# Scores of the first token tile with both key halves side by side, and rotary scores with the halves stacked on the partitions

## The chip, the cores and the metric

The kernel runs on one core of a Trainium2 chip. The core has five engines that work at the same time and wait for each other by semaphores: TensorE (PE; matmuls and transposes into PSUM), VectorE (DVE), ScalarE (ACT), GpSimd (POOL) and SyncE (SP, which here only starts transfers). Results of TensorE land in PSUM, which has eight banks of 128 partitions by 512 values; everything else is kept in SBUF. The metric is the device time in microseconds (us), the median of several runs.

## The reference

A decoder trunk of two layers over 256 tokens (one sequence, model width 2048), all in float32. Layer 0 is differential attention: 16 heads in pairs, each of 128 values per head, partial rotation, two softmaxes per pair whose difference weighs the values. Layer 1 is latent attention: queries and keys come out of low-rank projections; each of 16 heads has 128 unrotated values and 64 rotated ones, and the rotated key is one for all heads. Both are causal. After each of them comes a cross attention into 256 memory tokens and a squared-ReLU MLP of width 8192; a final norm closes the trunk. What matters here:

```python
# layer 0, per pair of heads
s = jnp.einsum('bqhcd,bkhcd->bhcqk', qi, k).astype(jnp.float32) * scale
s = jnp.where(causal_mask(q0, S), s, -jnp.inf)
p = jax.nn.softmax(s, axis=-1)
a = (p[:, :, 0] - lam * p[:, :, 1]).astype(v.dtype)
...
# layer 1
k_rope = apply_rope(d[..., MLA_Q_LORA + MLA_KV_LORA:][:, :, None, :], cos, sin)
q = jnp.concatenate([q[..., :MLA_NOPE], apply_rope(q[..., MLA_NOPE:], cos, sin)], axis=-1)
k = jnp.concatenate([kv[..., :MLA_NOPE],
                     jnp.broadcast_to(k_rope, (B, S, MLA_HEADS, MLA_ROPE))], axis=-1)
s = jnp.einsum('bqhd,bkhd->bhqk', qi, k).astype(jnp.float32) * scale
```

## The kernel before

**Precision.** Every operand of a float32 product is kept as two halves, a high one (the value rounded by a cast) and a low one (the rest, by a subtraction). A product is three matmuls into one PSUM bank: high by high, high by low, low by high. ScalarE makes the high half and VectorE the low half: of weights on lines 193 and 194 (`whi`, `wlo`, tiles of 128 x 1024, a ring of four buffers each, so that a cast waits until TensorE has used up an older weight), of activations in `split` (lines 296 and 297, tiles `unit`).

**Tiling.** The 256 tokens are two token tiles of 128, t = 0 and t = 1. The second tile sees 256 keys, the first one 128. Attention is worked in four groups of four heads (layer 0: four components, which is two pairs). A group is a Q, K and V projection, then scores, softmax, transposes of the probabilities, the weighted values, and the output projection of the group, which lies in the order behind the next group's start.

**Order of the work.** TensorE's order is written out by hand. The projections, which stream the weights, are the main line; scores, softmax, transposes are side tasks: generators that yield how long the next step should be put off (`T_ROT` = 12.0 for a rotation, `T_SM` = 6.5 for a softmax, `T_EV` = 2.6 for an evacuation), on a clock of the program's own to which each matmul adds its cost. `pump` runs between two pieces of the main line and takes a side step that is due; `need` runs side tasks until an operand exists. A side task that needs a PSUM bank takes one of four by `side_bank` and returns it with `give_back`. The order on VectorE, ScalarE, GpSimd and SyncE is set by the scheduler of the build, not by hand.

**Scores and softmax.** `scores` (line 530) writes the scores of four blocks of 128 keys (first tile) or two of 256 keys into one bank; VectorE adds the causal mask in place (line 541) and takes the maximum (line 511, `nmax`), ScalarE does the exponentials and row sums into an SBUF tile `p` (line 513), VectorE the reciprocal (line 518). In layer 1 (`attend4`) VectorE multiplies `p` by it (line 552), TensorE transposes `p` (line 159), and the transposes are split. In layer 0 (`attend_diff`) VectorE scales the two softmaxes of a pair into `a` (lines 641 and 642), and TensorE transposes `a`. The `ev` tiles, of which there are seven buffers, hold `p` and evacuated projections.

**The rotary part of layer 1.** `rotated` in `project_latent` evacuates the 64 rotary values of four heads by ScalarE (line 456, 128 x 256), GpSimd rotates them in place by six operations (`rope`, lines 467 to 472), TensorE turns two heads at a time (4 transposes for both token tiles), and `split` makes the halves. Two heads then lie one above the other on the partitions; the key `krope`, made by `shared_key`, has a copy for the upper and one for the lower position, with zeros in the other. So each rotary score is three products as well. The query projection and its evacuation (line 456, 128 x 512) follow the rotary projection, the transposes of the query follow these.

Of the kernel before, what the change touches and what calls it, by code (L numbers as in the profile page):

```python
# [10 lines left out]
F32 = mybir.dt.float32  # L11
# [6 lines left out]
P = 128  # L18
# [27 lines left out]
def trunk(ctx, tc, x, xT, xT0, mem, memT, positions, gcols, gfinal, lam_vecs, consts, W, out):  # L46
# [16 lines left out]
    def nm(s):  # L63
        serial[0] += 1
        return f"{s}_{serial[0]}"
# [104 lines left out]
    def raw_tile():  # L170
        return wraw.tile([P, 4 * CH], F32, tag="raw", name=nm("raw"))
# [333 lines left out]
    def softmax(sb, n):  # L505
# [4 lines left out]
        pr = work.tile([P, CH], F32, tag="ev", name=nm("p"), bufs=EVS)  # L510
        nc.vector.tensor_reduce(nmax[:, :n], sb.rearrange("p (n k) -> p n k", n=n), AX.X, ALU.max, negate=True)  # L511
        for i in range(n):
            nc.scalar.activation(  # L513
                pr[:, i * w : (i + 1) * w], sb[:, i * w : (i + 1) * w], AF.Exp,
                bias=nmax[:, i : i + 1], accum_out=ssum[:, i : i + 1],
            )
# [13 lines left out]
    def scores(sb, blocks, nk, t, causal):  # L530

        m = len(blocks)
        view = sb[:, : m * nk].rearrange("p (m k) -> p m k", m=m)
        for b, pairs in enumerate(blocks):
            n = len(pairs)
            for i, (q, qi, mh, ml) in enumerate(pairs):
                qs = slice(t * P, (t + 1) * P)
                mm3(view[:, b], q[:, 0, qi, qs], q[:, 1, qi, qs], mh, ml, i == 0, i == n - 1)
        if causal:
            last = view[:, :, nk - P :]  # L540
            nc.vector.tensor_tensor(last, last, mask.unsqueeze(1).broadcast_to([P, m, P]), ALU.add)

    def attend4(score_pairs, inputs, v, dst, causal):

# [1 line left out]
        pTs = [raw_tile().bitcast(F32R).rearrange("p (a b c d) -> p a b c d", a=2, b=2, c=2) for _ in range(2)]  # L546

        def probs(t, heads, nk):
            sb = yield from side_bank()
            scores(sb, [score_pairs(h, nk) for h in heads], nk, t, causal)  # L550
            pr, rs = softmax(sb, len(heads))
            nc.vector.tensor_tensor(
                pr.rearrange("p (h k) -> p h k", k=nk), pr.rearrange("p (h k) -> p h k", k=nk),
                rs[:, : len(heads)].unsqueeze(2).broadcast_to([P, len(heads), nk]), ALU.mult,
            )
# [69 lines left out]
    def attend_diff(q, k, v, dst, coef, subcols):  # L625


        def block(t, heads, out):
            nk = (t + 1) * P
            sb = yield from side_bank()  # L630
            comps = [s for h in heads for s in (2 * h, 2 * h + 1)]
            scores(sb, [[(q, s, k[:, 0, s, :nk], k[:, 1, s, :nk])] for s in comps], nk, t, True)
            n = 2 * len(heads)
            pr, rs = softmax(sb, n)
            nc.vector.tensor_tensor(rs[:, :n], rs[:, :n], coef[:, :n], ALU.mult)
            a = work.tile([P, S], F32, tag="a", name=nm("a"))
            for i in range(len(heads)):
                p0 = pr[:, 2 * i * nk : (2 * i + 1) * nk]
                p1 = pr[:, (2 * i + 1) * nk : (2 * i + 2) * nk]
                ai = a[:, i * nk : (i + 1) * nk]  # L640
                nc.vector.tensor_scalar(ai, p1, rs[:, 2 * i + 1 : 2 * i + 2], None, ALU.mult)
                nc.vector.scalar_tensor_tensor(ai, p0, rs[:, 2 * i : 2 * i + 1], ai, ALU.mult, ALU.add)
# [457 lines left out]
    def cross(l, norm, m, mk):  # L1100
        a = norm.done()
        rq = keep2(norm.rstd, SC_CA, "rq")
        q = Held(unit())
        ps = matmul_chunk(a)
        for t in range(NT):
            heads_T(ps[t], t, rq[t], q)
        o = Held(unit())
        mv = []
        attend4(
            lambda h, nk: [(q, h, mk[:, 0, h, :], mk[:, 1, h, :])], q.tasks + mk.tasks,  # L1110
            lambda: mv[0] if mv else None, o, False,
        )
        mv.append(mem_values(m))
        return project_out([o], G_MLP + 16 * l)
# [118 lines left out]
    acts = norm.done()  # L1233
    rk = keep2(norm.rstd, 1.0, "r1")
    hm = MLA_ROPE // 2
    krope = Held(raw_tile().bitcast(F32R)[:, : 4 * S].rearrange("p (a k t) -> p a k t", a=2, k=2))
    LAT = 3 * P

    def latent_piece(es, at, ps, lo, n):
# [35 lines left out]
    for t in range(NT):  # L1275
        e = work.tile([P, 2, P], F32, tag="a", name=nm("kr"))
        nc.vector.memset(e, 0.0)
        nc.scalar.activation(e[:, 0, 0:64], ps[t][:, 2 * P : 2 * P + 64], AF.Copy, scale=rk[t])
        ropes.append(e)
    ckv, rs = latent(ekv, G_KV)  # L1280
    rkv = keep2(rs, 1.0, "rkv")
# [1 line left out]
    def shared_key():  # L1283
        for t in range(NT):
            e = ropes[t]
            rope(e[:, 0:1, 0:64], cos[:, t, hd:], sin[:, t, hd:], 1, hm)
            nc.vector.tensor_copy(e[:, 1, 64:128], e[:, 0, 0:64])
        yield T_ROT
        b = yield from side_bank()
        for t in range(NT):  # L1290
            pt = b[:, 2 * t * P : 2 * (t + 1) * P]
            for i in range(2):
                flip(pt[:, i * P : (i + 1) * P], ropes[t][:, i, :])
        for t in range(NT):
            split(krope, t, b[:, 2 * t * P : 2 * (t + 1) * P].rearrange("p (k t) -> p k t", k=2))
        give_back()
        yield T_TURN

    def project_latent(gi):
        qr, q, k, v = Held(unit()[:, :, :2]), Held(unit()), Held(unit()), unit()  # L1300
        ps = matmul_chunk([cq], 256)

        def rotated(ps):
            es = []
            for t in range(NT):
                e = evacuate(ps[t][:, :256], rq[t])
                rope(e[:, :256].rearrange("p (h d) -> p h d", h=4), cos[:, t, hd:], sin[:, t, hd:], 4, hm)
                es.append(e)
            yield T_ROT
            b = yield from side_bank()  # L1310
            for t in range(NT):
                pt = b[:, 2 * t * P : 2 * (t + 1) * P]
                for i in range(2):
                    flip(pt[:, i * P : (i + 1) * P], es[t][:, i * P : (i + 1) * P])
            for t in range(NT):
                split(qr, t, b[:, 2 * t * P : 2 * (t + 1) * P].rearrange("p (k t) -> p k t", k=2))
            give_back()
            yield T_TURN

        qr.run(rotated(ps))  # L1320
# [139 lines left out]
```

## Time and profile before

| | us |
|---|---|
| median of 3 runs | 2239.43 (2238.33 to 2239.86) |
| profiled execution | 2237.86 |
| its span | 2236.1 |
| TensorE busy | 2215.5 (99%) |
| VectorE busy | 1744.0 (78%) |
| ScalarE busy | 1360.7 (61%) |
| GpSimd busy | 131.7 (6%) |

The granted TensorE clock was 0.999 over the span. In the rows of the profile PE, DVE, ACT, POOL and SP are the engines and L155 is line 155 of the kernel before. A row of the timeline has the start in us, the busy time, engine, line, operation, output tile <- input tiles, shapes and how many instructions follow each other (x12); in square brackets stands the idle time of the engine before it and what ended it. A row of the waits has an engine, line and tile, what it waited for, and the sum in us, the number of times and the longest. A row by form has the busy time, the mean duration in ns of one, and the idle time before. Consecutive matmuls overlap, so a duration is longer than the distance from one start to the next. Groups of layer 0 lie in the first 372 us (the fourth one's first tile at 346 to 361 us), those of layer 1 between about 1225 and 1420 us, the four groups' projections of the query at 1240, 1268, 1325 and 1378 us.

### The profile page before, as it was taken

The page shows a single profiled execution, that of the slowest core. Times are in us where ns is not written, and L with a number is a line of the kernel's source. Part 1 is how long each engine was busy: PE and PEld are TensorE (multiplying, and loading weights), DVE is VectorE, ACT ScalarE, POOL GpSimd, SP SyncE. Part 2 cuts the span into 40 slices and gives each one's busy share as a digit, 9 for nine tenths or more (in the row PEclk, how much of TensorE's full clock was granted, in tenths as well). Part 3 has the DMA queues.
Part 4 walks back from the last instruction along what each step waited for, and adds up shares of the span by engine and source line. Part 5 has one row for each costly group of instructions (what it writes and reads, how often), then busy time and mean ns, then how long its engine had stood idle before and what let it go on. Part 6 is the DMA issues. An engine that isn't in the chain of part 4 may idle for free.

```text
span 2236.1 us, 27352 instructions
## 1 busy us (share of the span) xinstructions
PE 2215.5 (99%) x10477; PEld 1847.1 (83%) x10477; DVE 1744.0 (78%) x1916; ACT 1360.7 (61%) x1815; POOL 131.7 (6%) x222
## 2 busy tenths in 40 slices
PE   9999999999999999999999999999999999999998
PEld 7888888888878888888889888888888888888886
DVE  6665748779889888889865767778988988898874
ACT  7544546666666666666655655566766666666664
POOL 1101010000000000000000311000000000000001
PEclk9999999999999999999999999999999999999999
DMA  9446555435766765766845244634666666677581
GB/s 385 169 151 221 178 194 204 164 127 193 253 201 211 258 209 215 247 214 213 262 170 185 94 160 160 237 132 151 215 254 226 195 253 226 196 253 227 194 281 57
DMA packets 69683, 454.73 MB, mean 203 GB/s; under 512 B 7984, under 2 KB 8368, under 8 KB 17584
## 3 DMA queue, kind: packets, MB, share of 16 engines
q1 hardware_dynamic: 65232, 423.09, 52.5%
q0 software_dynamic: 4032, 29.36, 7.2%
q8 instruction: 82, 1.34, 0.2%
q10 hardware_dynamic: 288, 0.52, 0.1%
q14 instruction: 49, 0.40, 0.1%
HBM read 450.85 MB, written 2.10 MB: 203 GB/s over the span
## 4 chain that ended last, share of the span: by engine, by line
PE 86%; DVE 8%; DMA 3%; issue 2%; ACT 1%; ACTq 0%; POOLq 0%; DVEq 0%
PE mm L155 61%; PE pr L155 19%; DVE wlo L194 4%; DMA raw<-in_mlp_wup_dram 3%; PE ax L155 3%; PE ax L159 2%; DVE raw L757 1%; PE mm L159 1%; ACT whi L193 1%; DVE unit L398 1%; DVE raw L425 0%; DVE x L451 0%; DMA raw<-in_da_wqkv_dram 0%; DVE p L809 0%; DVE raw L409 0%
## 5 line engine op out<-in xcount | busy, mean ns | idle before, releaser
L193 ACT CAST whi<-raw 128x1024 fp32r<-128x1024 f32 (+2 forms) x962 | 1000.1, 1041 | 735.8 <-PE mm L155 571.7
L155 PE MATMUL mm<-whi,unit 128*128 128x512 f32 (+3 forms) x4544 | 1438.7, 388 | 2.1 <-ACT unit L328 1.2
L194 DVE TENSOR_TENSOR wlo<-raw,whi 128x1024 fp32r<-128x1024 f32 (+2 forms) x962 | 1144.1, 1211 | 354.2 <-ACT whi L193 345.0
L155 PEld LDWEIGHTS mm<-whi,unit 128*128 128x128 f32 x4544 | 848.9, 188 | 168.0 <-ACT unit L328 2.1
L155 PE MATMUL mm<-wlo,unit 128*128 128x512 f32 (+3 forms) x2272 | 876.5, 386 | 3.1 <-DVE wlo L194 3.1
L155 PE MATMUL pr<-whi,unit 128*128 128x512 f32 x1568 | 505.6, 391 | 0.0
L155 PEld LDWEIGHTS mm<-wlo,unit 128*128 128x128 f32 x2272 | 427.3, 188 | 84.8 <-DVE wlo L194 6.0
L155 PEld LDWEIGHTS pr<-whi,unit 128*128 128x128 f32 x1568 | 294.4, 188 | 60.7
L155 PE MATMUL pr<-wlo,unit 128*128 128x512 f32 x784 | 306.2, 391 | 3.0 <-DVE wlo L194 2.9
L757 DVE TENSOR_TENSOR raw<-raw,raw 128x2048 f32<-128x2048 f32 x84 | 192.4, 2290 | 49.4 <-DMA raw<-in_mlp_wup_dram 49.2
L155 PEld LDWEIGHTS pr<-wlo,unit 128*128 128x128 f32 x784 | 147.3, 188 | 36.4 <-DVE wlo L194 6.5
L451 DVE TENSOR_TENSOR x<-x,mm 128x512 f32<-128x512 f32 x152 | 101.1, 681 | 14.3 <-PE mm L155 13.8
L749 POOL DMA_DIRECT2D raw<-in_mlp_wup_dram x28 | 24.5, 874 | 1109.6 <-DVE wlo L194 1109.6
L296 ACT CAST unit<-ax 128x512 fp32r<-128x512 f32 (+1 forms) x88 | 48.9, 566 | 30.4 <-PE ax L159 28.2
L340 POOL TENSOR_TENSOR rs<-rs,mhalf 128x1 f32<-128x1 f32 (+1 forms) x28 | 23.5, 844 | 708.2 <-DVE rs L339 708.2
L297 DVE TENSOR_TENSOR unit<-ax,unit 128x512 fp32r<-128x512 f32 (+1 forms) x88 | 57.6, 662 | 3.2 <-ACT unit L296 2.4
L1132 ACT ACTIVATE p<-p,r 128x512 f32<-128x512 f32 x56 | 40.5, 723 | 15.5 <-DVE p L809 15.0
L809 DVE TENSOR_TENSOR p<-pr,p 128x512 f32<-128x512 f32 x70 | 47.9, 684 | 0.8 <-PE pr L155 0.8
L159 PEld LDWEIGHTS ax<-identr,p 128*128 128x128 f32 x304 | 37.7, 139 | 9.8
L159 PE MATMUL ax<-identr,p 128*128 128x128 f32 x304 | 45.4, 272 | 0.0
L513 ACT ACTIVATE p<-ax,nmax 128x256 f32<-128x256 f32 (+1 forms) x80 | 33.6, 427 | 14.9 <-DVE nmax L511 14.6
L334 ACT ACTIVATE junk<-x 128x512 bf16<-128x512 f32 x56 | 35.1, 627 | 9.5 <-DVE x L451 8.4
(138 smaller groups left out, 907.1 us busy)
## 6 DMA issues: line engine op xcount, KB each, us to landing
raw<-in_mlp_wup_dram SPq DMA_DIRECT2D x128, 1024.0 KB, 5.0
raw<-in_mlp_wdown_dram SPq DMA_DIRECT2D x128, 1024.0 KB, 5.2
raw<-in_da_wqkv_dram SPq DMA_DIRECT2D x45, 1024.0 KB, 5.5
raw<-in_mlp_wup_dram POOLq DMA_DIRECT2D x28, 1024.0 KB, 8.4
raw<-in_da_wo_dram SPq DMA_DIRECT2D x16, 1024.0 KB, 4.9
raw<-in_ca_wkv_dram SPq DMA_DIRECT2D x16, 1024.0 KB, 5.0
raw<-in_mla_wo_dram SPq DMA_DIRECT2D x16, 1024.0 KB, 5.9
raw<-in_ca_wq_dram SPq DMA_DIRECT2D x8, 1024.0 KB, 5.8
```

The source lines that it names most:

```text
L155: return nc.tensor.matmul(o, stationary, moving, start=start, stop=stop)
L159: nc.tensor.transpose(o, src, ident)
L193: nc.scalar.copy(hi, r)
L194: nc.vector.tensor_tensor(lo, r, f32(hi), ALU.subtract)
L296: nc.scalar.copy(hi, src)
L297: nc.vector.tensor_tensor(dst[:, 1, :n, t * P : (t + 1) * P], src, f32(hi), ALU.subtract)
L334: nc.scalar.activation(junk[:, : src.shape[1]], src, AF.Square, accum_out=acc)
L451: nc.vector.tensor_tensor(xc, xc, ps, ALU.add)
L513: nc.scalar.activation(pr[:, i * w : (i + 1) * w], sb[:, i * w : (i + 1) * w], AF.Exp, bias=nmax[:, i : i + 1], accum_out=ssum[:, i : i + 1],)
L757: nc.vector.tensor_tensor(o, o, q, ALU.add)
L809: nc.vector.tensor_tensor(o, p, q, op)
L1132: nc.scalar.activation(r, src, AF.Relu, scale=rstd[t])
```

## The change

*Scores of the first tile.* For each half of the query one matmul runs over both halves of the key, 256 columns: the high and the low half of the 128 keys side by side. A block so takes 2 x 128 columns of PSUM, two blocks a bank, four blocks two banks (`side_banks(2)`). VectorE adds the mask to the half of the low keys, writing into the SBUF tile `p`, and then adds the half of the high keys; per bank two operations of 256 columns, where one of 512 columns for all four blocks stood. The maximum and the exponentials read `p`. This adds the product of the two low halves to the sum. The second tile and the cross attention keep three products with the terms listed out (`whole`).

*Rotary part.* After the rotation, ScalarE copies the high half of each head's 64 values into columns 0 to 63 of a tile `hl` (a new tile of the `ev` ring), and VectorE writes the low half into columns 64 to 127; after the transposes the high half of a head lies on partitions 0 to 63 and the low half on 64 to 127. That takes one transpose for each head and token tile, 8 instead of 4, in two banks one after the other. The result is copied by ScalarE alone, without a split. The key has its high half on both partition halves, once, and its low half on partitions 0 to 63 with zeros above. A rotary score is then two products (key high: gives high by high and low by high; key low), or one in the first tile, where the two key halves stand side by side. `T_ROT` becomes `T_ROT + 1.5` for the query.

```diff
+    def side_banks(n):
+        while free_banks[0] < n:
+            yield 0.5
+        free_banks[0] -= n
+        return [bank() for _ in range(n)]
...
+    def whole(q, k, h):
+        return [(q[:, 0, h], (k[:, 0, h], k[:, 1, h])), (q[:, 1, h], (k[:, 0, h],))]
+    def side_by_side(q, k, h):
+        both = k[:, :, h, :P]
+        return [(q[:, 0, h], both), (q[:, 1, h], both)]
...
+    def scores_of_first(sbs, blocks):
+        pr = work.tile([P, CH], F32, tag="ev", name=nm("p"), bufs=EVS)
+        for i, sb in enumerate(sbs):
+            view = sb.rearrange("p (m a k) -> p m a k", m=2, a=2)
+            for b in range(2):
+                todo = blocks[2 * i + b]
+                for j, (q, kk) in enumerate(todo):
+                    mmul(view[:, b], q[:, :P], kk, j == 0, j == len(todo) - 1)
+            o = pr[:, i * S : (i + 1) * S].rearrange("p (m k) -> p m k", m=2)
+            nc.vector.tensor_tensor(o, view[:, :, 1], mask.unsqueeze(1).broadcast_to([P, 2, P]), ALU.add)
+            nc.vector.tensor_tensor(o, o, view[:, :, 0], ALU.add)
+        return pr
...
         def block(t, heads, out):
-            sb = yield from side_bank()
-            scores(sb, [[(q, s, k[:, 0, s, :nk], k[:, 1, s, :nk])] for s in comps], nk, t, True)
-            pr, rs = softmax(sb, n)
+            if t == 0:
+                sb, other = yield from side_banks(2)
+                pr = scores_of_first([sb, other], [side_by_side(q, k, s) for s in comps])
+                give_back()
+                pr, rs = softmax(pr, n, pr)
+            else:
+                sb = yield from side_bank()
+                scores(sb, [whole(q, k, s) for s in comps], t, True)
+                pr, rs = softmax(sb, n)
...
     def shared_key():
-            rope(e[:, 0:1, 0:64], cos[:, t, hd:], sin[:, t, hd:], 1, hm)
-            nc.vector.tensor_copy(e[:, 1, 64:128], e[:, 0, 0:64])
+            rope(e[:, 1:2, 0:64], cos[:, t, hd:], sin[:, t, hd:], 1, hm)
+            for i in range(2):
+                nc.scalar.copy(e[:, 0, 64 * i : 64 * (i + 1)].bitcast(F32R), e[:, 1, 0:64])
+            nc.vector.tensor_tensor(e[:, 1, 0:64], e[:, 1, 0:64], e[:, 0, 0:64], ALU.subtract)
...
         def rotated(ps):
-                e = evacuate(ps[t][:, :256], rq[t])
-                rope(e[:, :256].rearrange("p (h d) -> p h d", h=4), cos[:, t, hd:], sin[:, t, hd:], 4, hm)
-                es.append(e)
-            yield T_ROT
+                e = evacuate(ps[t][:, :256], rq[t])[:, :256].rearrange("p (h d) -> p h d", h=4)
+                rope(e, cos[:, t, hd:], sin[:, t, hd:], 4, hm)
+                o = work.tile([P, 4, P], F32, tag="ev", name=nm("hl"), bufs=EVS)
+                nc.scalar.copy(o[:, :, 0:64].bitcast(F32R), e)
+                nc.vector.tensor_tensor(o[:, :, 64:], e, o[:, :, 0:64], ALU.subtract)
+                es.append(o)
+            yield T_ROT + 1.5
             for t in range(NT):
-                    flip(pt[:, i * P : (i + 1) * P], es[t][:, i * P : (i + 1) * P])
-            for t in range(NT):
-                split(qr, t, b[:, 2 * t * P : 2 * (t + 1) * P].rearrange("p (k t) -> p k t", k=2))
+                b = yield from side_bank()
+                for h in range(4):
+                    flip(b[:, h * P : (h + 1) * P], es[t][:, h, :])
+                nc.scalar.copy(qr[:, :, t * P : (t + 1) * P], b.rearrange("p (h t) -> p h t", h=4))
+                give_back()
...
     def attend_latent(held, o):
-            lambda h, nk: [
-                (q, h, k[:, 0, h, :nk], k[:, 1, h, :nk]),
-                (qr, h // 2, krope[:, 0, h % 2, :nk], krope[:, 1, h % 2, :nk]),
-            ],
+            lambda h, first: side_by_side(q, k, h) + [(qr[:, h], krope[:, :, :P])]
+            if first
+            else whole(q, k, h) + [(qr[:, h], (krope[:, 0], krope[:, 1]))],
```

More of the change, by code (lines that the diff above doesn't have):

```diff
@@ L503, in val, with softmax @@
         return v[:, half, 2 * kb : 2 * kb + 2, :].rearrange("p a b -> p (a b)")[:, lo : lo + n]
-    def softmax(sb, n):
+    def softmax(sb, n, pr=None):
         w = CH // n
@@ L509, in softmax @@
         ssum = small.tile([P, 4], F32, tag="ssum", name=nm("ssum"))
-        pr = work.tile([P, CH], F32, tag="ev", name=nm("p"), bufs=EVS)
+        if pr is None:
+            pr = work.tile([P, CH], F32, tag="ev", name=nm("p"), bufs=EVS)
         nc.vector.tensor_reduce(nmax[:, :n], sb.rearrange("p (n k) -> p n k", n=n), AX.X, ALU.max, negate=True)
@@ L528, in prob_T, with scores @@
         return o
-    def scores(sb, blocks, nk, t, causal):
+    def whole(q, k, h):
[3 more added lines that the diff above has]
+        return [(q[:, 0, h], both), (q[:, 1, h], both)]
+    def scores(sb, blocks, t, causal):
         m = len(blocks)
-        view = sb[:, : m * nk].rearrange("p (m k) -> p m k", m=m)
+        view = sb[:, : m * S].rearrange("p (m k) -> p m k", m=m)
+        qs = slice(t * P, (t + 1) * P)
         for b, pairs in enumerate(blocks):
[L535 to L538, printed above, removed]
+            todo = [(q[:, qs], kk) for q, ks in pairs for kk in ks]
+            for i, (q, kk) in enumerate(todo):
+                mmul(view[:, b], q, kk, i == 0, i == len(todo) - 1)
         if causal:
-            last = view[:, :, nk - P :]
+            last = view[:, :, S - P :]
             nc.vector.tensor_tensor(last, last, mask.unsqueeze(1).broadcast_to([P, m, P]), ALU.add)
+    def scores_of_first(sbs, blocks):
+        pr = work.tile([P, CH], F32, tag="ev", name=nm("p"), bufs=EVS)
+        for i, sb in enumerate(sbs):
[8 more added lines that the diff above has]
+        return pr
     def attend4(score_pairs, inputs, v, dst, causal):
@@ L548, in probs @@
         def probs(t, heads, nk):
-            sb = yield from side_bank()
-            scores(sb, [score_pairs(h, nk) for h in heads], nk, t, causal)
-            pr, rs = softmax(sb, len(heads))
+            if nk == P:
+                sb, other = yield from side_banks(2)
+                pr = scores_of_first([sb, other], [score_pairs(h, True) for h in heads])
+                give_back()
+                pr, rs = softmax(pr, len(heads), pr)
+            else:
+                sb = yield from side_bank()
+                scores(sb, [score_pairs(h, False) for h in heads], t, causal)
+                pr, rs = softmax(sb, len(heads))
             nc.vector.tensor_tensor(
@@ L1109, in cross @@
         attend4(
-            lambda h, nk: [(q, h, mk[:, 0, h, :], mk[:, 1, h, :])], q.tasks + mk.tasks,
+            lambda h, first: whole(q, mk, h), q.tasks + mk.tasks,
             lambda: mv[0] if mv else None, o, False,
@@ L1290, in shared_key @@
         for t in range(NT):
[L1291 removed]
             for i in range(2):
[L1293 to L1295 removed]
+                flip(b[:, (2 * t + i) * P : (2 * t + i + 1) * P], ropes[t][:, i, :])
+        nc.scalar.copy(krope.tile.rearrange("p k (t c) -> p k t c", t=NT), b.rearrange("p (t k c) -> p k t c", t=NT, k=2))
         give_back()
```

16 lines of the change are left out of this document (7 added, 9 removed).

## The prediction

> **What bounds the kernel now.** I read the page first (busy shares and the chain that ended last), then TensorE's waits, its instructions by form, and the timelines of the places that the change touches.
>
> ```profile
> span 2236.1 us, 27352 instructions
> ...
> PE 2215.5 (99%) x10477; PEld 1847.1 (83%) x10477; DVE 1744.0 (78%) x1916; ACT 1360.7 (61%) x1815; POOL 131.7 (6%) x222
> ...
> PE 86%; DVE 8%; DMA 3%; issue 2%; ACT 1%; ACTq 0%; POOLq 0%; DVEq 0%
> ...
> PE mm L155 <- DVE wlo L194: 3.1, 6, 1.0
> ...
> PE ax L159 <- DVE a L642: 1.3, 1, 1.3
> ```
>
> TensorE is busy for 99% of the span and carries 86% of the chain. Its list of waits has eight rows, of which the first and the third are shown, and adds up to 11.4 us; in scores and softmax there is a single one of more than 1 us, at `a` of line 642. So a matmul less is time saved, and equally each microsecond by which a softmax or a rotation comes later than its transposes is time lost: TensorE runs its hand-written order and has nothing else to do at that point. The forecast is therefore one saving and a list of waits.
>
> **What TensorE saves.**
>
> ```profile
> L155 PE MATMUL ax<-unit,unit 128*128 128x256 f32 x144 | 22.3, 282 | 0.0
> L155 PE MATMUL ax<-raw,unit 128*128 128x128 f32 x96 | 15.1, 267 | 0.0
> L155 PE MATMUL ax<-unit,unit 128*128 128x128 f32 x96 | 13.6, 270 | 0.0
> ...
> 77.14 1.03 PE L159 MATMUL mm<-identr,ev 128*128 128x128 f32 x8
> 77.93 0.48 PE L155 MATMUL mm<-whi,unit 128*128 128x512 f32 x1
> ...
> 80.75 1.45 PE L155 MATMUL ax<-unit,unit 128*128 128x128 f32 x12
> 82.03 0.45 PE L155 MATMUL mm<-whi,unit 128*128 128x512 f32 x1
> ...
> 86.23 0.88 PE L155 MATMUL ax<-unit,unit 128*128 128x256 f32 x6
> 86.94 0.40 PE L155 MATMUL mm<-whi,unit 128*128 128x512 f32 x1
> ```
>
> From start to next start: 12 matmuls of 128 columns take 1.28 us (0.107 each), 6 of 256 columns 0.71 us (0.118 each), 8 transposes 0.79 us (0.099 each). Twice the columns cost a tenth more, so one 256-wide matmul over both key halves replaces two 128-wide ones almost for the price of one. Differential attention: 16 components times 3 matmuls become 16 times 2. Latent attention, first tile: 16 heads times 6 become 16 times 3 (two for the unrotated part, one for the rotary part). Latent attention, second tile: 16 times 6 of 256 columns become 16 times 5. In all 48 + 96 = 144 matmuls of 128 columns go (15.4 us); 32 + 48 of 256 columns come and 16 go, net 64 more (7.6 us); the rotary query is turned in 8 transposes per group and token tile pair instead of 4, 16 more in all (1.6 us). Saved: 15.4 - 7.6 - 1.6 = 6.2 us. That the strided 256 columns (two halves apart in the tile) stream at another rate than contiguous ones no row shows; at 0.107 for a half, twice, they would cost 80 times 0.096 = 7.7 us more, and with that the saving would be gone. I take the contiguous row, because it is the same operand type and width.
>
> **What VectorE and ScalarE get.** VectorE: per first tile one mask addition of 512 columns becomes two of 256 and two more additions of 256, 8 times; 10 subtractions come (`hl`, `kr`), 10 go. ScalarE: 11 instructions more. Against 22% and 39% of idle time this is nothing by its sum; the price is in the order. Both run what they issue in order, and the order of the built program shows where the new `hl` copy, which waits for GpSimd's rotation, or the longer softmax, stands in front of work that TensorE waits for. I laid each such place out by hand with durations from the rows. GpSimd's and SyncE's orders don't change.
>
> *Differential attention, fourth group.*
>
> ```profile
> 352.95 0.36 ACT L513 ACTIVATE p<-ax,nmax 128x128 f32<-128x128 f32 x1
> 355.50 1.05 ACT L193 CAST whi<-raw 128x1024 fp32r<-128x1024 f32 x1 [1.06 <-issue]
> 358.97 1.04 ACT L193 CAST whi<-raw 128x1024 fp32r<-128x1024 f32 x1 [1.50 <-PE mm L155]
> 359.70 0.61 DVE L642 SCALAR_TENSOR_TENSOR a<-p,rsum,a 128x128 f32<-128x128 f32 x2
> 360.20 0.50 PE L159 MATMUL ax<-identr,a 128*128 128x128 f32 x2 [1.32 <-DVE a L642]
> 360.89 1.22 DVE L194 TENSOR_TENSOR wlo<-raw,whi 128x1024 fp32r<-128x1024 f32 x1
> ```
>
> Here the wait exists already, 1.32 us. In the new order the maximum stands behind a weight's low half and two residual additions, the four exponentials behind the cast that started at 355.50, and the scaling into `a` behind the weight whose cast started at 358.97 (it waits for TensorE, so it can't be earlier): 360.0 for that cast, 1.1 for the weight's low half, 0.6 for the next maximum, 1.3 for the scaling: `a` at 363.1 instead of 360.2. **+3.0** (2 to 4.5). In the first three groups TensorE had no wait here (the list has this one alone), and I put them at nothing.
>
> *Latent attention, first group's query.*
>
> ```profile
> 1233.96 0.53 POOL L467 TENSOR_TENSOR rope<-ev,cos 128x128 f32<-128x128 f32 x1 [3.58 <-ACT ev L456]
> 1236.89 0.69 ACT L456 ACTIVATE ev<-mm,rq 128x512 f32<-128x512 f32 x1 [0.30 <-PE mm L155]
> 1238.54 1.44 POOL L472 TENSOR_TENSOR ev<-rope,rope 128x128 f32<-128x128 f32 x1
> 1239.21 0.68 ACT L456 ACTIVATE ev<-mm,rq 128x512 f32<-128x512 f32 x1
> 1243.60 0.46 POOL L472 TENSOR_TENSOR ev<-rope,rope 128x128 f32<-128x128 f32 x1
> ...
> 1240.78 1.03 PE L159 MATMUL ax<-identr,ev 128*128 128x128 f32 x8
> ```
>
> Before, the two query evacuations (1236.89, 1239.21) run while GpSimd rotates (first token tile until 1240.0, second until 1244.1), and the transposes at 1240.78 start with no wait. In the new order ScalarE has: first tile's `hl` copy (waits for that tile's rotation), the second tile's evacuation, two weight casts, second tile's `hl` copy (waits for the second rotation), and only then the two query evacuations. GpSimd's second rotation can't start before its evacuation, at about 1240; it took 4.1 us, so 1244.1, the copy 0.4 (as the cast of 256 columns at 1253.00, quoted below), the evacuations until 1245.0 and 1245.6: **+4.4** (3 to 5.5).
>
> *Third and fourth group's query.*
>
> ```profile
> 1317.78 1.13 POOL L467 TENSOR_TENSOR rope<-ev,cos 128x128 f32<-128x128 f32 x1 [49.01 <-ACT ev L456]
> 1321.69 1.44 POOL L472 TENSOR_TENSOR ev<-rope,rope 128x128 f32<-128x128 f32 x1
> 1321.83 0.69 ACT L456 ACTIVATE ev<-mm,rq 128x512 f32<-128x512 f32 x1 [0.31 <-PE mm L155]
> 1324.15 0.68 ACT L456 ACTIVATE ev<-mm,rq 128x512 f32<-128x512 f32 x1
> 1326.32 0.46 POOL L472 TENSOR_TENSOR ev<-rope,rope 128x128 f32<-128x128 f32 x1
> ...
> 1325.72 1.03 PE L159 MATMUL ax<-identr,ev 128*128 128x128 f32 x8
> 1378.88 1.03 PE L159 MATMUL ax<-identr,ev 128*128 128x128 f32 x8
> ```
>
> The same pattern. First rotation until 1323.1 (5.35 us), or 1322.1 if the weight's low half that slows its last step (1.44 against 0.46 us) is held up too; copy and second evacuation 0.8; second rotation 3.7 us, to 1326.7 or 1327.6; copy, evacuation: 1327.7 to 1328.7, against transposes at 1325.72. **+2.5** (1.75 to 3.7). In the fourth group the rows are the same 53 us later (transposes at 1378.88); **+2.5**.
>
> [...]
>
> *Latent attention's softmax.*
>
> ```profile
> 1253.00 0.36 ACT L296 CAST raw<-ax 128x256 fp32r<-128x256 f32 x1
> 1254.40 0.28 PE L155 MATMUL mm<-whi,unit 128*128 128x256 f32 x1
> ...
> 1258.87 0.37 ACT L513 ACTIVATE p<-ax,nmax 128x128 f32<-128x128 f32 x1 [2.77 <-DVE nmax L511]
> 1260.25 0.85 ACT L456 ACTIVATE ev<-mm,rq 128x256 f32<-128x256 f32 x2
> 1260.62 0.69 DVE L552 TENSOR_TENSOR p<-p,rsum 128x512 f32<-128x512 f32 x1
> 1264.26 0.90 POOL L472 TENSOR_TENSOR ev<-rope,rope 128x128 f32<-128x128 f32 x1
> 1265.61 0.60 PE L159 MATMUL ax<-identr,p 128*128 128x128 f32 x4
> ```
>
> In the first group `p` is done 4.3 us before its transposes. In the new order the next group's rotation is drawn ahead: its evacuation comes before the exponentials, the first `hl` copy between them, and the product of line 552 waits behind the second `hl` subtraction. GpSimd's two rotations of about 4 and 3.5 us one after the other, with an evacuation between, end some 9 us after the last matmul of the 256-column projection (1254.40), and copy, subtraction and product add 1.5: 1265.7, against transposes that move up to 1263.9 (1.2 us of the scores are saved, and 0.4 us of matmuls fewer lie between). **+1.8**, taken as 2 (1 to 4). Fourth group: four exponentials behind two casts that wait for TensorE, by the same reckoning **+1.8** (1 to 2.5). Second and third: room left, 0.2 together (0 to 0.5).
>
> **The sum.** Waits 3.0 + 4.4 + 2.5 + 2.5 + 2.0 + 1.8 + 0.2 = 16.4; minus 6.2: +10.2 us. The profiled execution took 2237.86 us, 1.6 us under the median of 2239.43 us, so its sum is 2248.1, and on the median 2249.6. I say 2249. All lower ends together (11.0) give +4.8, all upper ends (24.4) +18.2.
>
> **The rivals.** (a) The waits don't come: GpSimd is faster where the held-up casts no longer make VectorE collide with it, ScalarE reaches the copies with the rotation done, and what is left hides in the 2 to 4 us of room. For it: a rotation step takes 0.46 us alone, so a rotation takes 2.7 us instead of 5.35. Against it: even then, at the third group, 2.7 + 0.8 + 2.7 + 0.9 from 1317.78 is 1324.9, which just meets the transposes at 1325.72; so it needs all steps at their fastest. Then the saving decides: 2239.4 - 6.2 = 2233. (b) Half the waits come: 6 to 8 us against 6.2, the time stays within 4.5 us of before, 2240. (c) All upper ends, or strided columns at twice the price: 2257. (d) VectorE becomes the bound: 22 instructions more of some 0.4 us are 9 us in 2236, with 22% idle; no.
>
> [...]
>
> **Chances.** Forecast (waits at several places, +4.5 to +14) 0.64; (c) 0.15; (b) 0.12; (a) 0.09. The range takes (c) and the upper part of (b): 2241 to 2257. A measurement of this kernel can tell about 0.2%, 4.5 us, from no change. Faster by more 0.09, within it 0.12, slower 0.79.
>
> **What would show it.** In the changed profile: TensorE's instruction sum down by 6 us; transposes of `ev` in latent attention waiting 2 to 5 us for an evacuation that follows directly on an `hl` copy on ScalarE, whose own wait is for GpSimd; transposes of `a` in differential attention's fourth group waiting about 4.4 us; `p` of the first and fourth latent group about 2 us. Wrong would be: these waits absent; 256-wide score matmuls in the first tile above 0.15 us from start to start; new waits for weights, if ScalarE's casts stand too long behind an `hl` copy.

## The result, and the profile after

The changed kernel takes 2259.62 us (median of 5 runs, 2254.98 to 2260.63), the kernel before 2239.26 us: ratio 1.0086, interval 1.0072 to 1.0101, so 20.4 us slower. The direction was as forecast; 2249 was forecast, and 2257 was the upper end.

The page of the changed kernel, the lines that answer to those of before:

```profile
span 2253.1 us, 27247 instructions
...
PE 2215.5 (98%) x10413; PEld 1846.3 (82%) x10413; DVE 1751.6 (78%) x1938; ACT 1367.9 (61%) x1826; POOL 131.7 (6%) x222
...
PE 87%; DVE 7%; DMA 2%; issue 2%; POOL 1%; ACT 1%; POOLq 0%; ACTq 0%; DVEq 0%
```

TensorE has fewer instructions and is busy for just as long, 2215.5 us, and the span is 17 us longer. Both need an explanation. The profiled execution took 2254.98 us, the fastest of the five.

TensorE's waits in the changed kernel (what waited <- for what: us in all, times, longest):

```profile
PE ax L165 <- ACT ev L462: 10.9, 3, 4.9
PE ax L165 <- DVE a L686: 4.2, 1, 4.2
PE ax L165 <- DVE rsum L525: 3.8, 1, 3.8
PE pr L161 <- DVE wlo L200: 2.6, 3, 1.5
PE ax L165 <- DVE p L590: 1.9, 1, 1.9
```

Six waits at transposes, 20.8 us, where the kernel before had one of 1.3 us. They stand at the places that the prediction named: three queries' evacuations (`ev`), `a` in differential attention's fourth group, and the softmax of the first and the fourth latent group (`rsum` and `p`).

The other part is the clock. Stretches of 4 us around the wait for `a`; after the span's length the columns are busy time (and instructions) of TensorE, its weight loads, VectorE, ScalarE, GpSimd, then the granted clock, the DMA share and GB/s:

```profile
353.00:357.00 4.00, 4.00 (x21) 3.16 (x19) 4.00 (x6) 3.33 (x13) 0.00 (x0) 1.00 0.48 182
357.00:361.00 4.00, 0.09 (x1) 0.00 (x0) 4.00 (x13) 2.04 (x6) 0.00 (x0) 1.00 0.10 17
361.00:365.00 4.00, 3.75 (x11) 3.01 (x12) 3.75 (x12) 2.18 (x7) 0.00 (x0) 0.57 0.35 116
365.00:369.00 4.00, 4.00 (x24) 3.37 (x22) 1.92 (x4) 2.27 (x6) 0.54 (x1) 1.00 0.74 254
```

TensorE stands still in the second stretch, and in the third it works at a clock of 0.57: 11 instructions where 21 and 24 fit before and after. So the wait of 4.2 us is followed by more than 3 us of work at half speed (a clock of 0.50 from 361.02 to 364.41 us). The busy time hides this: it counts the slow matmuls as busy, 3.75 us for 11 of them, which is why it did not fall.

How one query wait comes about, first latent group. ScalarE's, GpSimd's and TensorE's timeline of the changed kernel:

```profile
1240.31 0.41 ACT L1356 CAST hl<-ev 128x256 fp32r<-128x256 f32 x1 [3.05 <-POOL ev L478]
1240.62 0.47 ACT L462 ACTIVATE ev<-mm,rq 128x256 f32<-128x256 f32 x1
1245.43 0.41 ACT L1356 CAST hl<-ev 128x256 fp32r<-128x256 f32 x1 [2.89 <-POOL ev L478]
1245.74 1.26 ACT L462 ACTIVATE ev<-mm,rq 128x512 f32<-128x512 f32 x2
...
1241.23 0.46 POOL L473 TENSOR_TENSOR rope<-ev,cos 128x128 f32<-128x128 f32 x1 [0.96 <-ACT ev L462]
1244.95 0.45 POOL L478 TENSOR_TENSOR ev<-rope,rope 128x128 f32<-128x128 f32 x1
...
1246.48 1.97 PE L165 MATMUL ax<-identr,ev 128*128 128x128 f32 x8 [4.87 <-ACT ev L462]
1248.10 0.78 PE L161 MATMUL mm<-whi,unit 128*128 128x512 f32 x1
1251.66 0.74 PE L161 MATMUL mm<-whi,unit 128*128 128x512 f32 x2
```

ScalarE stands idle for 3.05 and 2.89 us with a copy at its head that waits for GpSimd, the second time while the query's evacuation behind it could run (TensorE had started the query projection's last matmul at 1241.22); it starts 0.31 us after the second copy, and TensorE has waited 4.87 us for it. The slow clock after the wait: 8 transposes take 1.62 us until 1248.10 (0.79 in the kernel before), the next 8 matmuls 3.56 us until 1251.66, 0.445 each instead of 0.227. That is 2.6 us more on top of the 4.9; about 0.3 us of it follows a wait at full clock too (8 transposes in 1.00 us after a short wait, `wait_short` below).

What TensorE was to save is there. First the form, then the first score block:

```profile
L161 PE MATMUL ax<-unit,unit 128*128 128x256 f32 x208 | 32.7, 282 | 0.0
...
80.62 1.11 PE L161 MATMUL ax<-unit,unit 128*128 128x256 f32 x8
81.57 0.40 PE L161 MATMUL mm<-whi,unit 128*128 128x512 f32 x1
```

Eight matmuls over both key halves take 0.95 us, 0.119 each, as contiguous ones did (0.118); the block takes 0.33 us less than the 12 of before. The rival with strided columns at twice the price is out.

**The account** in the first profiled execution: -6.2 (saving) + 19.5 (waits, 20.8 - 1.3) + 6.9 (slow clock, the excess of TensorE's start-to-start distances in the microseconds after each wait over those at full speed, less some 0.3 us each that a wait at full clock has behind it too) = +20.2 us. Against the kernel before's profiled 2237.86 this execution is only 17.1 us longer. In the two lists of waits the rows of weight halves and first units are some 2.3 us smaller (3.1 + 2.9 + 1.2 against 1.9 + 2.6 + 0.4); such rows move by a microsecond or two from one kernel here to the next. The remaining 0.8 us is not assigned.

### The profile page after: what moved, and what is told of

Its sections match the earlier page's. It is cut to its first block, busy times and chain, and to the rows that moved or that the text cites. A ratio compares the mean times of both kernels' runs of the same rounds, so it can differ in the third digit from the quotient of the medians.

```text
span 2253.1 us, 27247 instructions
## 1 busy us (share of the span) xinstructions
PE 2215.5 (98%) x10413; PEld 1846.3 (82%) x10413; DVE 1751.6 (78%) x1938; ACT 1367.9 (61%) x1826; POOL 131.7 (6%) x222
## 4 chain that ended last, share of the span: by engine, by line
PE 87%; DVE 7%; DMA 2%; issue 2%; POOL 1%; ACT 1%; POOLq 0%; ACTq 0%; DVEq 0%
PE mm L161 61%; PE pr L161 20%; DVE wlo L200 4%; PE ax L165 2%; PE ax L161 2%; DMA raw<-in_mlp_wup_dram 2%; PE mm L165 1%; DVE raw L801 1%; ACT whi L199 1%; DVE unit L404 0%; DVE raw L431 0%; DVE x L457 0%; POOL rope L475 0%; POOL ev L478 0%; DVE p L853 0%
## 5 line engine op out<-in xcount | busy, mean ns | idle before, releaser
L302 ACT CAST unit<-ax 128x512 fp32r<-128x512 f32 x80 | 46.1, 587 | 25.9 <-PE ax L165 25.9
L303 DVE TENSOR_TENSOR unit<-ax,unit 128x512 fp32r<-128x512 f32 x80 | 54.1, 684 | 3.2 <-ACT unit L302 2.5
L1176 ACT ACTIVATE p<-p,r 128x512 f32<-128x512 f32 x56 | 40.5, 722 | 10.9 <-DVE p L853 10.4
L1177 ACT ACTIVATE p<-p 128x512 f32<-128x512 f32 x56 | 35.4, 631 | 1.1
```

Source lines behind the costliest of these rows:

```text
L303: nc.vector.tensor_tensor(dst[:, 1, :n, t * P : (t + 1) * P], src, f32(hi), ALU.subtract)
L1176: nc.scalar.activation(r, src, AF.Relu, scale=rstd[t])
L1177: nc.scalar.activation(r, r, AF.Square)
```

## The experiments

The theory: the time goes into six waits that come from the order on ScalarE and VectorE, and into the half-speed clock after those that are long. The rivals: the new instructions themselves cost it, wherever they stand; or the waits follow the rotation on GpSimd and cannot be moved; or the clock has nothing to do with the waits. All times beside "before" are of the same chip.

### Each half of the change alone

Scores side by side with the rotary part of before (`scores_only`), the core of the edit against the changed kernel:

```diff
-                o = work.tile([P, 4, P], F32, tag="ev", name=nm("hl"), bufs=EVS)
-                nc.scalar.copy(o[:, :, 0:64].bitcast(F32R), e)
-                nc.vector.tensor_tensor(o[:, :, 64:], e, o[:, :, 0:64], ALU.subtract)
...
-            lambda h, first: side_by_side(q, k, h) + [(qr[:, h], krope[:, :, :P])]
+            lambda h, first: side_by_side(q, k, h)
+            + [(qr[:, 0, h // 2], krope[:, :, h % 2, :P]), (qr[:, 1, h // 2], krope[:, :, h % 2, :P])]
...
```

> Only the first tile's scores side by side; the rotary part with its splits as before. Theory (the time is lost where TensorE waits behind the new order on ScalarE and VectorE, and in the half-speed clock after long waits): the three query waits (4.9, 3.0, 3.0 us) are absent, the wait for a in differential attention's fourth group stays at about 4.2 us with some 1.5 us of slow matmuls after it; saved 16 x 0.085 + 16 x 0.17 = 4.1 us; sum 4.3 - 4.1, about 0: 2238 to 2242. Rival (the 256-wide matmuls over two halves and VectorE's additions are themselves what costs): about 2255 or more.

Rotary halves stacked, scores of the first tile as before (`rotary_only`):

```diff
-            if nk == P:
-                sb, other = yield from side_banks(2)
-                pr = scores_of_first([sb, other], [score_pairs(h, True) for h in heads])
-                give_back()
-                pr, rs = softmax(pr, len(heads), pr)
...
+            sb = yield from side_bank()
+            scores(sb, [score_pairs(h, False) for h in heads], t, causal, nk)
+            pr, rs = softmax(sb, len(heads))
...
```

> Only the rotary halves stacked; the first tile's scores as before (three products, one bank, mask in place). Theory: all three query waits (4.9, 3.0, 3.0 us) are there, with about 1.5 us of slow clock after two or three of them, perhaps the first latent group's softmax too (3.8 us); the wait for a stays at 1.3 us as in the kernel before; saved only 2.0 us: 2250 to 2258. Rival (the side-by-side scores cost): within 3 us of 2239.

Measured: `scores_only` 2237.06 us against 2238.9 (ratio 0.9988, 0.9979 to 0.9997); `rotary_only` 2256.26 (1.0072, 1.0055 to 1.0089). `scores_only` lies 1 us under its range. The scores' half loses nothing in the sum: the wait at `a`, 4.2 us instead of 1.3, and some 2.5 us of slow clock behind it (a mean clock of 0.997, 0.999 in the kernel before) stand against a saving of some 4 us and 1.3 us less of waits for weight halves and first units. The rotary half carries nearly all of the loss, with query waits of 10.9 us and a softmax wait of 3.1 us.

### The copies later in the program, and the transposes put off

The same work, with the copies issued some 10 us after the rotation (`hl_later`):

```diff
-            es = []
+            es, hs = [], []
...
                 rope(e, cos[:, t, hd:], sin[:, t, hd:], 4, hm)
+                hs.append(e)
+            yield 11.0
+            for e in hs:
                 o = work.tile([P, 4, P], F32, tag="ev", name=nm("hl"), bufs=EVS)
                 nc.scalar.copy(o[:, :, 0:64].bitcast(F32R), e)
                 nc.vector.tensor_tensor(o[:, :, 64:], e, o[:, :, 0:64], ALU.subtract)
                 es.append(o)
-            yield T_ROT + 1.5
+            yield 4.0
```

(and the same for `kr`, 10 us and 3 us).

> The whole change, but the copies into high and low halves are issued some 10 us after the rotation instead of right behind it, so that they stand behind the query's evacuations on ScalarE. Theory: the three query waits go, and with them their slow clock; what stays is the wait for a (4.2 us and 1.5 us of slow clock) and perhaps the fourth latent group's softmax (2 us): 2236 to 2243. Rival (the added work itself, wherever it stands): no change against the changed kernel, 2255 or more.

Then also the transposes put off (`all_later`):

```diff
-            yield T_SM + (0.8 if causal else 0.0)
+            yield T_SM + ((3.8 if nk == P else 0.8) if causal else 0.0)
...
-            yield T_SM + 4.3
+            yield T_SM + (8.8 if t == 0 else 4.3)
```

> As before this one, and the transposes of a (first tile, differential attention) and of p (first tile, latent attention) put off by 4.5 and 3 us in the order of TensorE. Theory: no wait above 1 us left in scores and softmax, the clock at full speed there, the saving of 6.2 us and the 1.3 us of the old wait are kept: 2231 to 2234. Rival: 2255 or more; or the waits only move to the later steps (weighted values), 2238 or more.

Measured: `hl_later` 2240.79 against 2238.9 (1.0012, 1.0001 to 1.0023), 1.9 us over the kernel before where the changed kernel with the same instructions is 20.4 over: the rival that they cost by themselves is out. `all_later` 2237.32 (0.999, 0.9981 to 0.9999), which misses the 2234. The wait for `a` did not go; it fell only from 4.2 to 3.5 us, with a stretch of half clock still behind it (a mean clock of 0.998, against 0.999 before), and three waits for evacuations, of up to 1.2 us, were left. VectorE's timeline of `all_later`:

```profile
363.55 1.23 DVE L200 TENSOR_TENSOR wlo<-raw,whi 128x1024 fp32r<-128x1024 f32 x1
364.69 0.49 DVE L685 TENSOR_SCALAR a<-p,rsum 128x128 f32<-128x128 f32 x2
365.21 0.62 DVE L686 SCALAR_TENSOR_TENSOR a<-p,rsum,a 128x128 f32<-128x128 f32 x2
```

With the transposes 4.5 us later in TensorE's order, the build's scheduler put more work ahead of the scaling, another weight's low half among it; `a` is done at 365.8, where the changed kernel had it at 361 (quoted below). So a time written into TensorE's order does not fix what VectorE does before it.

### ScalarE's order, or GpSimd's rotation

The changed kernel with one word replaced (`hl_on_dve`):

```diff
-                nc.scalar.copy(o[:, :, 0:64].bitcast(F32R), e)
+                nc.vector.tensor_copy(o[:, :, 0:64].bitcast(F32R), e)
```

> The changed kernel with the query's high-half copy after the rotation on VectorE instead of ScalarE, at the same place in the program: ScalarE's query evacuation no longer stands behind a copy that waits for GpSimd, VectorE's weight halves do. Theory (the three query waits come from ScalarE's order, which it keeps): they shrink from 10.9 us to under 3 us in all, and what VectorE now holds up is partly covered by the ring of four weights: 2240 to 2250. Rival (the waits follow GpSimd's rotation itself): query waits of 3 us each stay, 2256 or more.

Measured: 2242.52 us against 2240.3 (1.0013, 1.0003 to 1.0023), 17 us under the changed kernel on that chip (2259.35). The waits of `hl_on_dve`:

```profile
PE ax L165 <- DVE p L590: 4.8, 2, 2.9
PE ax L165 <- DVE a L686: 4.2, 1, 4.2
...
PE ax L165 <- ACT ev L462: 1.3, 1, 1.3
```

The query waits fall from 10.7 to 1.3 us, with the rotation and the copy where they were in the program. What made them was that the copy stood at the head of ScalarE. VectorE now waits in ScalarE's place, and the query's transposes need nothing that stands behind the copy there; the first group's `p` does stand behind it, and its wait, 3.7 us before, is 2.9.

### The wait for `a` by itself

The changed kernel with the fourth group's first tile in differential attention as before (`da4_old`):

```diff
     def attend_diff(q, k, v, dst, coef, subcols):
+        diffs[0] += 1
+        beside = diffs[0] < 4
...
-            if t == 0:
+            if t == 0 and beside:
                 sb, other = yield from side_banks(2)
...
```

> The changed kernel, with the first tile's scores of differential attention's fourth group alone as before (three products, one bank). Theory: the wait for a falls from 4.2 to 1.3 us and the slow clock after it (1.5 us) goes, 0.1 us of saving is lost: 4.3 us less than the changed kernel, 2254 to 2256. Rival (this wait is made up for later): within 1.5 us of the changed kernel.

and the changed kernel once more (`after_again`):

> The changed kernel once more, for a second trace. Theory (whether the clock falls after a wait of about 3 us is a matter of where the wait lies in time, not of the program): the same waits to 0.1 us (4.2, 4.9, 3.8, 3.0, 3.0, 1.9); the slow clock after the first three each time, after the two of 3.0 us in either, both or none, which is 1.5 us each in the time; 2255 to 2261. Rival (the fall belongs to the place): slow after the third group's wait and not after the fourth's, as in the first trace.

Measured: `after_again` 2259.35 us, `da4_old` 2252.02, both against 2240.3 (1.0083, 1.0065 to 1.0101, and 1.0054, 1.0038 to 1.0070). The difference is 7.3 us where 4.3 was expected, and 2252.02 lies under the range. In the traces of the two, the wait for `a` falls by 2.9 us, and the slow clock after it, 2.6 us in `after_again`, is gone (the mean clock is 0.996 instead of 0.994). The remaining 1.8 us is not assigned: the slow stretch behind the fourth latent group's query wait (1.6 us) is in `after_again` alone, but the one behind the first query is 0.8 us longer in `da4_old`. So the wait and its clock cost about 5.5 us by the traces, and the rival that they are made up for later is out.

The fourth latent group's query wait is the same 3.02 us in both traces of the changed kernel. The first trace, and the second one (`after_again`), each with the stretch of 4 us behind it:

```profile
1396.83 1.23 PE L165 MATMUL ax<-identr,ev 128*128 128x128 f32 x8 [3.02 <-ACT ev L462]
...
1398.00:1402.00 4.00, 4.00 (x19) 3.29 (x18) 2.47 (x4) 3.09 (x6) 0.00 (x0) 1.00 0.00 0
```

```profile
1397.73 1.24 PE L165 MATMUL ax<-identr,ev 128*128 128x128 f32 x8 [3.02 <-ACT ev L462]
...
1398.00:1402.00 4.00, 4.00 (x16) 3.14 (x15) 2.42 (x3) 2.78 (x5) 0.00 (x0) 0.63 0.01 4
```

One program, one place, one length of wait; once the clock stays at 1.00 and once it falls to 0.63. The rival that the fall belongs to the place is out. Part of the spread of the changed kernel's own runs (2255 to 2260.6 us) may come from this; only two executions have a trace, and these differ by 1.5 us in slow clock.

### The clock by itself

The kernel before, with the first query evacuation of the third and fourth latent group repeated 5 or 9 times on ScalarE into a tile that nobody reads (`wait_short`, `wait_long`):

```diff
         ps = matmul_chunk([cq])
+        if gi >= 2:
+            junk = work.tile([P, CH], F32, tag="ev", name=nm("junk"), bufs=EVS)
+            for _ in range(9):
+                nc.scalar.activation(junk, ps[0], AF.Copy, scale=rq[0])
```

> The kernel before, with the first query evacuation of the third and fourth latent group preceded by 5 repetitions of itself on ScalarE (some 0.57 us each, 2.9 us in all, of which 0.9 us is room): TensorE waits about 2 us at two places. Theory (a wait up to 2 us costs itself, a wait over 3 us costs also some 1.5 us of half-speed clock): 2 x 2 us, 2243, no slow matmuls after the waits. Rival (the clock falls at any wait, or not at all): with any wait 2246.

> As before this one with 9 repetitions: TensorE waits about 4.3 us at two places, 4.6 us more in all than with 5. Theory: 2 x (4.3 + 1.5 to 2.5) = 11.6 to 13.6 us, 2251 to 2253, with the 512-column matmuls after each wait at about 430 instead of 227 ns for 3 to 5 us. Rival (a wait costs only itself): 2 x 4.3, 2247.5, and the matmuls after it as fast as ever.

TensorE's timeline of `wait_long`, then of `wait_short`, third group:

```profile
1330.95 1.97 PE L159 MATMUL ax<-identr,ev 128*128 128x128 f32 x8 [4.71 <-ACT ev L456]
1332.57 0.78 PE L155 MATMUL mm<-whi,unit 128*128 128x512 f32 x1
...
1336.13 0.80 PE L155 MATMUL mm<-whi,unit 128*128 128x512 f32 x2
```

```profile
1328.77 1.24 PE L159 MATMUL ax<-identr,ev 128*128 128x128 f32 x8 [1.03 <-ACT ev L456]
1329.77 0.47 PE L155 MATMUL mm<-whi,unit 128*128 128x512 f32 x1
```

With none of the change in it, a wait of 4.71 us is followed by 8 matmuls in 3.56 us, 0.445 each; the first five after a wait of 1.03 us take 1.23 us, 0.25 each. Times: 2253.31 and 2244.71 us against 2239.85 (1.0064, 1.0049 to 1.0079, and 1.0022, 1.0012 to 1.0031). Not all fits: the short waits came out at 1.0 us, not 2, so `wait_short` should have been at 2242; two of the 2.7 us too much stand in its list as waits for weights (4.9 against 2.9 us). Between the two kernels the waits differ by 7.3 us and the times by 8.6, with 1.1 us less of weight waits in the longer, so 2.4 us is left for the clock; the trace of `wait_long` shows 3.7 us. That it costs time is shown; its size by this pair only within a microsecond or so.

### A version that beats both

The changed kernel with later copies, the first tile's transposes of `p` 3 us later, `a`'s where they were, and the fourth group's first tile in differential attention as before (`mixed`; the edits are those shown). `mixed13` has `yield 13.0` for both the 11 and the 10 us.

> The change with the copies issued later and p's transposes (first tile, latent attention) put off by 3 us, differential attention's transposes where they were, and its fourth group's first tile with three products as before. Theory (only the waits stand against the saving): the wait for a is back at 1.3 us with no slow clock after it, no wait above 1.4 us elsewhere in attention; saved 6.2 less 0.4 for that group: 2233 to 2236. Rival (something else of the new scores costs time too): 2239 or more.

> As mixed, with the copies of query and key another 2 and 3 us later. Theory: the waits for the key's and second query's evacuations that were left (0.8 to 1.4 us) go too: 2232 to 2235. Rival: the first group's scores now wait for the rotary key, and the wait comes back there: 2236 or more.

Measured: `mixed` 2235.16 us against 2239.85 (0.9982, 0.9973 to 0.9992), `mixed13` 2233.07 (0.9969, 0.9958 to 0.9980). The transposes' waits of `mixed13`:

```profile
PE ax L165 <- DVE a L690: 1.3, 1, 1.3
...
PE ax L165 <- DVE hl L1367: 1.0, 2, 0.7
...
PE ax L165 <- ACT ev L462: 0.7, 1, 0.7
```

No wait of a transpose above the old 1.3 us is left, the mean clock is 0.999 over the span, as in the kernel before, and the kernel is 6.8 us faster than the one before: the saving of 6.2 less 0.3 for the one group, within the interval (4.5 to 9.4 us). So the idea pays what TensorE's rows said; the order made it a loss.

## Why the prediction was wrong

**The saving, 6.2 us: right.** Shown by the distances of 0.119 us and by `mixed13`. The sign that was named for it, TensorE's instruction sum down by 6 us, did not come (2215.5 us twice), since that sum counts half-speed matmuls in full.

**The places of the waits: right, all six, and no other above 1 us.** The three query waits of the sum (4.4 + 2.5 + 2.5) rest on ScalarE's copy not being passed by a ready evacuation behind it, which no row of the kernel before shows. The changed kernel's trace shows it here: 2.89 us idle with the copy at the head, and the evacuation 0.31 us behind the copy. VectorE did the same at an `hl` subtraction of the first latent group: it stood idle for 1.24 us until 1269.38, and the maximum behind it, whose scores had been masked by 1268.14, came at 1269.72.

**Their sizes: 16.4 forecast, 19.5 measured.** `a` 3.0, measured 2.9 (4.2 - 1.3); first query 4.4, measured 4.9; third and fourth 2.5 each, measured 3.0 each; fourth group's softmax 1.8, measured 1.9; second and third group's softmax 0.2, measured 0. The wait for `a` came as laid out: scaling behind a weight's low half and the next maximum.

```profile
358.26 1.23 DVE L200 TENSOR_TENSOR wlo<-raw,whi 128x1024 fp32r<-128x1024 f32 x1
359.40 0.69 DVE L518 TENSOR_REDUCE nmax<-ax 128x2 f32<-128x512 f32 x1
360.85 1.00 DVE L686 SCALAR_TENSOR_TENSOR a<-p,rsum,a 128x128 f32<-128x128 f32 x3
...
361.25 0.74 PE L165 MATMUL ax<-identr,a 128*128 128x128 f32 x2 [4.16 <-DVE a L686]
```

The one that is well off is the first latent group's softmax, 2.0 forecast and 3.8 measured. The changed kernel there:

```profile
1263.14 0.28 PE L161 MATMUL ax<-raw,unit 128*128 128x256 f32 x1
1263.26 0.28 PE L161 MATMUL mm<-whi,unit 128*128 128x256 f32 x1
...
1264.24 0.48 ACT L462 ACTIVATE ev<-mm,rq 128x256 f32<-128x256 f32 x1 [1.08 <-PE mm L161]
1268.94 0.41 ACT L1356 CAST hl<-ev 128x256 fp32r<-128x256 f32 x1 [2.99 <-POOL ev L478]
1273.55 0.41 ACT L1356 CAST hl<-ev 128x256 fp32r<-128x256 f32 x1 [1.33 <-POOL ev L478]
...
1274.33 0.69 DVE L590 TENSOR_TENSOR p<-p,rsum 128x512 f32<-128x512 f32 x1
...
1275.16 0.63 PE L165 MATMUL ax<-identr,p 128*128 128x128 f32 x4 [3.75 <-DVE rsum L525]
```

The chain is as long as I had it: from the evacuation's start at 1264.24 to `p` at 1275.0 it is 10.8 us (11.0 forecast). But I had started it from the end of the projection in the kernel before, where the scores stand behind the projection. In the new order they stand inside it: the scores are through at 1263.26, and the projection goes on for more than a microsecond after them. So the rotation begins later against the scores, and their transposes come sooner.

**The step that failed: the sum had no term for TensorE's clock.** It counted a wait as its own length, "each microsecond by which a softmax or a rotation comes later than its transposes is time lost". By the measured waits alone the changed kernel would have come out at 2239.3 - 6.2 + 19.5 = 2252.6, within the range. The slow stretches, 6.9 us in the first trace and 8.4 in the second, took it out. The page of the kernel before could not show this: it has a clock of 0.999, and its list has no wait longer than 1.3 us. The runs show what was missing: in all traces of kernels with such waits, those of 3.5 us and more had a slow stretch behind them that cost 1.2 to 2.6 us, those of 3.0 and 3.1 us sometimes one of some 1.5 us and sometimes none, and those of 2.9 us and less none. In the first trace of the changed kernel the clock was 0.50 behind the waits of 4.16, 4.87, 3.75 and one of 3.02 us, and 1.00 behind the other of 3.02 and the one of 1.90 us. The forecast itself had waits of 4.4 us at `a` and at the first query, and by its ranges up to 3.7 us at the other two queries, lengths that had a slow stretch behind them wherever they came.

**The chances.** The lower ends add up to 10.5 us, not 11.0, so the lowest sum was +4.3; nothing hangs on that. "Slower" at 0.79 was right. The range's upper end, 2257, took all waits at their longest and no clock; the measured time came from waits near the forecast and the clock. That rival (c) lay nearest was by a cause that did not occur: the waits were not at their upper ends (24.4 us), and the strided columns run at the contiguous price (0.119 and 0.118 us).

## What to carry to other kernels

When work is inserted that waits for a slow engine, look at what stands behind it on its own engine's queue; the same copy issued 10 us later in the program, or on another engine, was worth 17 to 19 us here, and the instructions themselves cost nothing that could be measured. When a change makes the bounding engine wait, price the wait twice: its length, and the slow clock after it (here 1.2 to 2.6 us behind each wait of 3.5 us and more, and some 1.5 us behind some of those of 3.0), which the busy time counts as work. And a saving on the bounding engine should be booked only together with a list of what is late next.

## What the runs showed that was not expected

A wait of 3.0 us at one and the same place lets the clock fall in one execution and not in another: over the four traces that have this wait in the third and the fourth latent group (two of the changed kernel, `rotary_only`, `da4_old`) it fell 5 times in 8, always in the third, once in the fourth (0.63 in `after_again`, where the first trace has 1.00). The wait of 2.9 us in the trace of `hl_on_dve` and all shorter ones left it alone, but that is the only one between 1.9 and 3.0 us, and of ten executions of `hl_on_dve`, with mean clocks of 0.996 to 0.998, the traced one has 0.998.

What sets the one case apart from the other no run shows by itself. Where the clock falls and comes back can be read in a trace if the stretches are cut finely enough. First trace of the changed kernel, three slow stretches:

```profile
361.02:364.41 3.39, 3.16 (x9) 2.50 (x10) 3.25 (x11) 2.16 (x7) 0.00 (x0) 0.50 0.40 135
1245.07:1251.88 6.81, 5.40 (x17) 4.63 (x18) 2.18 (x5) 4.11 (x10) 3.14 (x13) 0.50 0.32 135
1340.65:1344.04 3.39, 3.39 (x12) 2.87 (x11) 2.42 (x3) 1.90 (x3) 0.00 (x0) 0.50 0.26 111
```

With the one behind the softmax's wait, the four slow stretches behind waits in this trace start at 361.01, 1245.06, 1275.78 and 1340.64 us and last 3.41, 6.83, 3.41 and 3.41 us; the starts lie 884.05, 30.72 and 64.85 us apart, to within 0.1 us 259, 9 and 19 times 3.413 us, the length of the short ones. An estimate from these numbers and from the waits of the same trace: if the time is laid off from these starts in steps of that length, the waits of 4.16, 4.87 and 3.75 us and the 3.02 us of the third group fill 0.8 to all of the step ahead of the fall, and the 3.02 us of the fourth group (1393.81 to 1396.83 us) fill 0.42 and 0.46 of two steps and the 1.90 us at most 0.44 of one, with no fall. So where a wait lies in time may decide beside its length. That fits the six waits of this trace; no run sets it by itself.

The two traced executions of the changed kernel differ by some 1.5 us in slow clock, and a mean clock of 0.995 instead of 0.999 on the whole span went with four such falls in the first trace, 0.994 with five in the second.
